# Neighbourhood attention in an encoder trunk: two key blocks laid over each other in PSUM, put apart again by GpSimd, and two PSUM pools in the other order

## The chip, the cores and the metric

The kernel runs on one core of a Trainium2 chip. The engines that matter are TensorE (PE in the profile, its weight loads PEld), VectorE (DVE), ScalarE (ACT), GpSimd (POOL) and SyncE (SP, which here issues most DMAs). The metric is the device time of one execution in microseconds (us); lower is better.

## The reference, cut to what matters

The trunk has two layers over 1024 tokens of width 1024, in float32. Layer 0 uses mixer A, layer 1 mixer B. The change touches mixer A: attention of 16 heads of 64 on a grid of 16 rows by 64 columns, in which each query sees a window of 8 rows and 16 columns of keys, clamped at the edges.

```python
def mixer_a(h, w_in, rpb, w_out):
    proj = h @ w_in
    q, k, v, gate = jnp.split(proj, 4, axis=-1)
    ...
    def row_block(args):                       # one grid row of queries
        kg = jnp.take(k, flat, axis=2)...      # the window's 8 x 16 keys
        sc = jnp.einsum('bhqd,bhqnd->bhqn', qb, kg) * scale
        sc = sc + bias                         # learned, by row and column offset
        pr = jax.nn.softmax(sc, axis=-1)
        return jnp.einsum('bhqn,bhqnd->bhqd', pr, vg)
    ...
    return (o * jax.nn.silu(gate)) @ w_out

for i in range(2):
    x = x + (mixer_a if i == 0 else mixer_b)(rms_norm(x, g[i]), ...)
    x = x + sigmoid(rms_norm(x, pg[i]) @ w_gate[i]) * (p[i] @ w_proj[i])
```

## The kernel before

**Stages.** The program runs mixer A (with the first layer's norm and projections), then `dense_phase(0)` (output projection, per-layer embedding gate), mixer B, and `dense_phase(1)`. Each stage opens its own PSUM pools; as pools are closed and opened, the banks of the eight pass from one stage to the next, and the first tile in a bank waits for the last reader of the tile that was there.

**Tiles of mixer A.** A token tile holds 128 tokens: all 16 grid rows of 8 neighbouring columns. So tile j's queries need keys of tiles j-1, j and j+1 alone. Every value is split into a high and a low part (fp32r), so a product is three matmuls, or two where the parts are stacked in the 128 rows of the array.

**One step** is one head h and one query tile j; there are 16 x 8 = 128 steps, and in 96 of them (j = 1 to 6) there are three key tiles. For a step the kernel issues:
- `f_S`: two matmuls of 384 columns give the scores in PSUM; one DVE operation (L741) adds the table `TB[h]` (bias and mask, negated) to them, writes `sp` to SBUF and keeps the smallest value;
- `f_E`: ACT takes the exponential of `sp` (L750) with the row's sum;
- `f_T`: PE transposes `sp` in blocks of 128 (L758, three of them, two at the edges), ACT copies the result from PSUM to `PTh` (L761) and DVE writes the rest to `PTl` (L762);
- `f_AV`: for key tile kb, PE multiplies the transposed weights of up to three query tiles with `V`.

**Order of the work.** In step n the list `att` takes `f_T(n)`, `f_E(n+1)`, `f_S(n+2)` and `f_AV(n-2)`, in that order. `mix` spreads between them the dense matmuls of the next head's query and key projection (`qk_items`) and of the gate. In heads 3, 7 and 11 the projection of V for the next four heads rides along with `f_AV`. After the last step two `f_AV` remain.

**Work held back.** `post.add(k, f)` holds a piece of work back by k ticks of the walk through the list, `later.add` by steps. The query and key projection of a head's half leaves PSUM by ACT into `th`; then at the ticks `QD = (2, 5, 8)` the functions `one`, `two` and `three` of `qk_evac` make `QS`, `KA` and `KB`: ACT copies (L685, L686), DVE subtractions (L689, L690) and two DVE copies from partitions 64 to 127 to partitions 0 to 63 (L691 for `KA`, L694 for `KB`).

**The end of a head** (`head_end`): when a half of a head's output is complete, ACT and DVE take it to `Y`, the row sums' reciprocals go through DRAM and come back by DMA as `rb`, and after the odd head of a pair `fin` multiplies on GpSimd `Y` by the gate (L563) and by `rb` (L564); then `split` writes high and low parts (ACT L560, DVE L561).

**GpSimd in mixer A** has the table of the next head (L716, five operations a head, at j = 1), the two multiplications of `fin`, and DMA issues of the weight sums (L632, `jobs`, at most one a step). Its queue runs in order: an operation that waits holds back all that follow.

**The dense phase's pools.** `ps_t` (transposes, 4 banks) is opened before `ps_d` (products, 4 banks), so `ps_t` has banks 0 to 3 and `ps_d` banks 4 to 7. Mixer A has its `d` in banks 0 and 1, `s` in 2 and 3, `t` in 4 and 5, `o` in 6 and 7. Mixer B has `d` in bank 0, `s` in 1 to 4, `t` in 5 and 6, `o` in 7.

Of the kernel before, what the change touches and what calls it, by code (L numbers as in the profile page):

```python
# [44 lines left out]
QD = (2, 5, 8)  # L45
# [42 lines left out]
def lay_out(inp):  # L88
# [47 lines left out]
    mask = np.where(ok, 0.0, BIG).astype(np.float32)  # L136

# [8 lines left out]
    def swap(v):  # L146
# [6 lines left out]
        "mask": mask, "rope": np.stack([cosT, sinT], axis=1),  # L153
# [5 lines left out]
def trunk(ctx, tc, x, wts, rpb, gains, hgains, mask, rope, gain0, out):  # L159
# [482 lines left out]
    def mixer_a():  # L642
        jobs = weight_sums()
        with ExitStack() as es:
# [6 lines left out]
            MK = one.tile([128, 5, 128], F32, name="MK")  # L651

# [19 lines left out]
            def qk_evac(h, hf):  # L672
                def evac(ps):
                    if hf == 0:
                        QS[h] = qkp.tile([128, 1024], F32R, name="QS")
                        KA[h] = qkp.tile([128, 1024], F32R, name="KA")
                        KB[h] = qkp.tile([128, 1024], F32R, name="KB")
                    s = slice(hf * 512, (hf + 1) * 512)
                    lo, hi = slice(0, 64), slice(64, 128)
                    qs, ka, kb = QS[h], KA[h], KB[h]  # L680
                    raw = sb.tile([128, 512], F32, name="th", bufs=2)
                    act.activation(raw, ps, AF.Copy)

                    def one():
                        act.activation(qs[lo, s], raw[lo], AF.Copy, scale=-0.125)  # L685
                        act.activation(ka[hi, s], raw[hi], AF.Copy)  # L686

                    def two():
                        dve.scalar_tensor_tensor(qs[hi, s], raw[lo], -0.125, qs[lo, s], op0=ALU.mult, op1=ALU.subtract)  # L689
                        dve.tensor_tensor(kb[hi, s], raw[hi], ka[hi, s], ALU.subtract)  # L690
                        dve.tensor_copy(ka[lo, s], ka[hi, s])  # L691

                    def three():
                        dve.tensor_copy(kb[lo, s], kb[hi, s])  # L694
                    for i, f in enumerate((one, two, three)):
                        if h == 0:
                            f()
                        else:
                            post.add(QD[i], f)
                return evac  # L700
# [19 lines left out]

            def near(j):
                return max(j - 1, 0), min(j + 1, NT - 1)

            def f_S(h, j):
                k0, k1 = near(j)
                n = (k1 - k0 + 1) * 128
# [3 lines left out]
                mm(ps[:, :n], qt, KA[h][:, ks], True, False)  # L730
                mm(ps[:, :n], qt, KB[h][:, ks], False, True)
# [14 lines left out]
            def f_E(h, j):  # L746
                k0, k1 = near(j)
                n = (k1 - k0 + 1) * 128
                sp, mn = SP[h, j]
                act.activation(sp[:, :n], sp[:, :n], AF.Exp, bias=mn, scale=-1.0, accum_out=RS[h][:, j:j + 1])  # L750

            def f_T(h, j):
                k0, k1 = near(j)
                m = k1 - k0 + 1
                sp, _ = SP.pop((h, j))
                ps = psT.tile([128, 4, 128], F32, name="t")
                for i in range(m):
                    pe.transpose(ps[:, i], sp[:, i * 128:(i + 1) * 128], ident)  # L758
                f0 = k0 * 3 + (j - k0 + 1)
                sl = slice(f0, f0 + 2 * m - 1, 2)  # L760
                act.activation(PTh[:, sl], ps[:, :m], AF.Copy)  # L761
                dve.tensor_tensor(PTl[:, sl], ps[:, :m], PTh[:, sl], ALU.subtract)  # L762
# [127 lines left out]
            sync.dma_start(MK, mask)  # L890
            for c in range(8):
                sync.dma_start(U[:, c], rpb[:, :, 7 - c:31 - c])
# [28 lines left out]
            PTh = ptp.tile([128, NT * 3, 128], F32R, name="PTh")  # L921
            PTl = ptp.tile([128, NT * 3, 128], F32R, name="PTl")
# [10 lines left out]
            f_E(0, 0)  # L933
            f_S(0, 1)
# [9 lines left out]
            for h in range(NH):  # L944
                att = []
                for j in range(NT):
                    n = h * NT + j
                    def head(h=h, j=j):
                        later.tick()
                        if j == 1 and h + 1 < NH:  # L950
                            table(h + 1)
                        if h >= 1 and j != 1 and jobs:
# [9 lines left out]
                    if n >= 2:  # L962
                        att += av_and_v(*steps[n - 2])
# [5 lines left out]
                if h == NH - 1:  # L969
                    att += [(lambda: f_AV(NH - 1, NT - 2), CA[4]), (lambda: f_AV(NH - 1, NT - 1), CA[4])]  # L970
# [517 lines left out]
    def dense_phase(l):  # L1488
        with ExitStack() as es:
            one = es.enter_context(tc.tile_pool(name="done", bufs=1))  # L1490
            ps_t = es.enter_context(tc.tile_pool(name="dpt", bufs=4, space=PSUM))
            ps_d = es.enter_context(tc.tile_pool(name="dps", bufs=4, space=PSUM))
# [250 lines left out]
NAMES = ["x", "wts", "rpb", "gains", "hgains", "mask", "rope", "gain0"]  # L1743
# [15 lines left out]
```

## Time and profile before

| | |
|---|---|
| median of 3 runs (lowest to highest) | 1531.45 us (1528.62 to 1531.79) |
| the profiled execution's own time, its span | 1530.75 us, 1528.9 us |
| granted TensorE clock, mean over the span | 0.998 |
| busy, share of the span: PE, PEld | 98%, 86% |
| DVE, ACT, POOL | 72%, 59%, 20% |
| mixer A's steps | about 60 to 530 us |
| `dense_phase(0)` | about 530 to 710 us |
| mixer B | about 710 to 1340 us |
| `dense_phase(1)` | about 1340 us to the end |

A group's row gives line, engine, operation, output and inputs by name, shape and count, then the busy time in us and the mean of one in ns, then the idle time before them and what ended it. In a timeline row stand the start in us, the duration in us, and in brackets the idle time before it and its releaser. Matmuls are pipelined: the duration of one runs from its start to the modelled end of its results, so two neighbours overlap, and what one costs on PE is the distance from its start to the next one's.

### The profile page before, as it was taken

What the parts mean: (1) busy time and instruction counts of PE and PEld (TensorE: products, weight loads), DVE (VectorE), ACT (ScalarE), POOL (GpSimd) and SP (SyncE); (2) the same over time, 40 slices, a digit from 0 to 9 for tenths busy, and PEclk for the clock granted to TensorE, in tenths of its full rate; (3) what the DMA queues carried; (4) which work ended last, traced back from release to release, by engine and by line L of the source; (5) the groups of instructions that cost most, each with busy time, mean ns of one, the idle gap of its engine ahead of it and who ended that gap; (6) DMA issues with size and microseconds to landing.
All of it is one profiled execution on the core that took longest, in us unless ns stands there. A gap on an engine that the chain in (4) does not pass through costs nothing.

```text
span 1528.9 us, 24361 instructions
## 1 busy us (share of the span) xinstructions
PE 1499.4 (98%) x8976; PEld 1314.0 (86%) x8976; DVE 1102.1 (72%) x2091; ACT 899.4 (59%) x1801; POOL 304.4 (20%) x413
## 2 busy tenths in 40 slices
PE   8999999999999999999999999999999999999997
PEld 8888988988988888888988889989899888878786
DVE  7566576477477599767887786777877877789856
ACT  6565465466366635433467676676767777745432
POOL 1222232142112000010222132453141300000022
PEclk9999999999999999999999999999999999999999
DMA  8325355272122962262210111111101122763123
GB/s 256 119 95 140 83 142 162 63 165 85 36 87 66 334 247 97 90 201 79 77 49 21 32 39 50 46 32 43 58 27 47 37 77 70 234 225 115 67 88 134
DMA packets 91096, 157.22 MB, mean 103 GB/s; under 512 B 18144, under 2 KB 54112, under 8 KB 90464
## 3 DMA queue, kind: packets, MB, share of 16 engines
q1 hardware_dynamic: 85824, 139.66, 27.9%
q0 software_dynamic: 2560, 8.39, 3.2%
q10 hardware_dynamic: 2592, 7.61, 1.4%
q8 instruction: 71, 1.16, 0.3%
q14 instruction: 49, 0.40, 0.1%
HBM read 125.10 MB, written 50.83 MB: 115 GB/s over the span
## 4 chain that ended last, share of the span: by engine, by line
PE 80%; DVE 11%; ACT 5%; issue 2%; DMA 1%; SPq 0%; ACTq 0%; DVEq 0%
PE d L317 50%; PE o L317 10%; PE s L317 8%; PE t L1214 6%; PE t L758 3%; DVE PTl L1217 2%; PE t L317 1%; PE t L467 1%; DVE mn L1198 1%; DVE xn L1541 1%; ACT PTh L1216 1%; ACT P L1204 1%; ACT wh L226 1%; DVE X L1437 1%; DVE HTl L1383 1%
## 5 line engine op out<-in xcount | busy, mean ns | idle before, releaser
L317 PE MATMUL d<-wh,HTh 128*128 128x256 f32 (+1 forms) x1032 | 343.3, 335 | 6.0 <-DVE HTl L469 2.3
L317 PE MATMUL d<-wh,HTl 128*128 128x256 f32 (+1 forms) x1032 | 338.3, 330 | 0.3 <-DVE HTl L469 0.3
L317 PE MATMUL d<-wl,HTh 128*128 128x256 f32 (+1 forms) x1032 | 337.0, 328 | 0.0
L1217 DVE TENSOR_TENSOR PTl<-t,PTh 128x512 fp32r<-128x512 f32 x256 | 164.4, 683 | 111.4 <-ACT PTh L1216 111.1
L317 PEld LDWEIGHTS d<-wh,HTh 128*128 128x128 f32 x1032 | 195.1, 190 | 25.8 <-DVE HTl L469 2.5
L317 PEld LDWEIGHTS d<-wl,HTh 128*128 128x128 f32 x1032 | 194.9, 190 | 19.0
L317 PEld LDWEIGHTS d<-wh,HTl 128*128 128x128 f32 x1032 | 195.1, 190 | 18.7 <-DVE HTl L469 0.5
L317 PE MATMUL d<-HTh,wh 128*128 128x512 f32 x504 | 206.0, 409 | 0.0
L317 PE MATMUL d<-HTh,wl 128*128 128x512 f32 x504 | 198.3, 394 | 0.0
L317 PE MATMUL d<-HTl,wh 128*128 128x512 f32 x504 | 197.6, 392 | 0.0
L1204 ACT ACTIVATE P<-s,mn 128x1024 f32<-128x1024 f32 x128 | 142.8, 1116 | 67.5 <-DVE mn L1198 66.7
L1216 ACT ACTIVATE PTh<-t 128x512 fp32r<-128x512 f32 x256 | 139.7, 593 | 45.1 <-PE t L1214 44.6
L1198 DVE TENSOR_REDUCE mn<-s 128x1 f32<-128x1024 f32 x128 | 154.7, 1209 | 12.3 <-PE s L317 12.3
L1214 PE MATMUL t<-ident,P 128*128 128x128 f32 x1024 | 137.2, 275 | 4.8 <-DVE PTl L1217 1.7
L317 PE MATMUL s<-KA,QS 128*128 128x512 f32 (+2 forms) x384 | 133.7, 402 | 0.0
L1214 PEld LDWEIGHTS t<-ident,P 128*128 128x128 f32 x1024 | 114.7, 140 | 20.1 <-DVE PTl L1217 12.6
L231 DVE TENSOR_TENSOR wl<-wstage,wh 128x1024 fp32r<-128x1024 f32 x78 | 101.7, 1308 | 34.7 <-ACT wh L226 34.2
L317 PE MATMUL s<-KB,QS 128*128 128x512 f32 (+2 forms) x384 | 121.8, 371 | 0.0
L317 PE MATMUL o<-PTh,V 128*128 128x256 f32 (+2 forms) x672 | 118.9, 288 | 1.2 <-DVE Y L483 0.9
L317 PE MATMUL o<-PTl,V 128*128 128x256 f32 (+2 forms) x672 | 119.1, 288 | 0.1
L762 DVE TENSOR_TENSOR PTl<-t,PTh 128x384 fp32r<-128x384 f32 (+1 forms) x128 | 66.6, 520 | 71.3 <-ACT PTh L761 70.1
L317 PEld LDWEIGHTS d<-HTh,wl 128*128 128x128 f32 x504 | 94.7, 188 | 21.6
(237 smaller groups left out, 2700.9 us busy)
## 6 DMA issues: line engine op xcount, KB each, us to landing
wstage<-in_wts SPq DMA_DIRECT2D x88, 512.0 KB
pp<-ppD SPq DMA_DIRECT2D x32, 256.0 KB
X<-in_x SPq DMA_DIRECT2D x15, 512.0 KB
rb<-rD SPq DMA_DIRECT2D x56, 128.0 KB
ppD<-th SPq DMA_DIRECT2D x20, 256.0 KB
tD0t<-in_wts SPq DMA_DIRECT2D x16, 256.0 KB
tD1t<-in_wts SPq DMA_DIRECT2D x16, 256.0 KB
xD<-X SPq DMA_DIRECT2D x8, 512.0 KB
```

Of the source, the lines that this page charges most:

```text
L226: act.activation(hi, s, AF.Copy)
L231: eng.tensor_tensor(lo[:, c:c + n], s[:, c:c + n], hi[:, c:c + n], ALU.subtract)
L317: pe.matmul(ps, a, b, start=first, stop=last, skip_group_check=True)
L467: pe.transpose(ps[:, k], xn[:, (4 * c + k) * 128:(4 * c + k + 1) * 128], ident)
L758: pe.transpose(ps[:, i], sp[:, i * 128:(i + 1) * 128], ident)
L762: dve.tensor_tensor(PTl[:, sl], ps[:, :m], PTh[:, sl], ALU.subtract)
L1198: dve.tensor_reduce(mn, ps, axis=AX.X, op=ALU.min)
L1204: act.activation(p, ps, AF.Exp, bias=mn, scale=-1.0, accum_out=RS[h, hf][:, t:t + 1])
L1214: pe.transpose(ps[:, i], p[:, k * 128:(k + 1) * 128], ident)
L1216: act.activation(PTh[:, ks, c], ps, AF.Copy)
L1217: dve.tensor_tensor(PTl[:, ks, c], ps, PTh[:, ks, c], ALU.subtract)
L1383: dve.tensor_tensor(al(t + m, c), src[m], ah(t + m, c), ALU.subtract)
```

## The change

**Overlay.** A key in tile j-1 (left) counts for a query only if its column within the tile is greater than the query's, a key in tile j+1 (right) only if it is smaller. For one pair of column numbers at most one of the two counts. The change uses this: after the scores' matmuls (still 384 columns) a new DVE operation copies the right block over the left one in PSUM, where a predicate (`SIDE[:, 2]`) says so (L747). The table of a head is joined in the same way, once a head (`join`, L726). The bias, the exponential, the transposes, `PTh` and `PTl` then handle 256 columns instead of 384 in the 96 inner steps; `sp` is 256 wide.

**Apart.** The transposed overlay lands in a staging slot of `PTh` and `PTl` (slots 24 and 25, by turns). Two GpSimd operations a step (L776, one for `PTh`, one for `PTl`) multiply it by two masks of ones and zeros into the two slots of the left and the right key tile. That is 192 operations more.

**AV later.** `f_AV` and the projection of V that rides with it run for step n-3 instead of n-2, and three `f_AV` remain after the last step. All that follows the end of a head comes one step later too.

**Query and key.** `QD` has five ticks instead of three. The two DVE copies across partitions (L691, L694 before) become ACT copies (L697), each at a tick of its own.

**Pools.** `ps_d` is opened before `ps_t`, so `ps_d` has banks 0 to 3 and `ps_t` banks 4 to 7.

The predicate tile `SIDE` (128 x 384) comes in by one more DMA at the start. Lines after the first hunk move down, by 1 to 20.

```diff
-QD = (2, 5, 8)
+QD = (2, 4, 6, 7, 9)
...
+    sides = np.stack([c[:, None] >= c[None, :], c[:, None] < c[None, :], c[:, None] > c[None, :]], axis=1).astype(np.float32)
...
+            SIDE = one.tile([128, 3, 128], F32, name="SIDE")
...
-                    def two():
+                    def low_q():
                         dve.scalar_tensor_tensor(qs[hi, s], raw[lo], -0.125, qs[lo, s], op0=ALU.mult, op1=ALU.subtract)
+
+                    def low_k():
                         dve.tensor_tensor(kb[hi, s], raw[hi], ka[hi, s], ALU.subtract)
-                        dve.tensor_copy(ka[lo, s], ka[hi, s])
-
-                    def three():
-                        dve.tensor_copy(kb[lo, s], kb[hi, s])
+
+                    def across(k):
+                        act.activation(k[lo, s], k[hi, s], AF.Copy)
+                    parts = (one, low_q, lambda: across(ka), low_k, lambda: across(kb))
...
+            def join(h):
+                dve.copy_predicated(TB[h][:, 1], SIDE[:, 2].bitcast(mybir.dt.int32), TB[h][:, 3])
...
-                    tb = TB[h][:, 1:4]
-                sp = sb.tile([128, 384], F32, name="sp", bufs=3)
+                    tb = TB[h][:, 1:3]
+                    dve.copy_predicated(ps[:, 0:128], SIDE[:, 2].bitcast(mybir.dt.int32), ps[:, 256:384])
+                sp = sb.tile([128, 256], F32, name="sp", bufs=3)
...
-                for i in range(m):
-                    pe.transpose(ps[:, i], sp[:, i * 128:(i + 1) * 128], ident)
-                f0 = k0 * 3 + (j - k0 + 1)
-                sl = slice(f0, f0 + 2 * m - 1, 2)
-                act.activation(PTh[:, sl], ps[:, :m], AF.Copy)
-                dve.tensor_tensor(PTl[:, sl], ps[:, :m], PTh[:, sl], ALU.subtract)
+                inner = 0 < j < NT - 1
+                for i in range(2):
+                    c = 1 - i if inner else i
+                    pe.transpose(ps[:, i], sp[:, c * 128:(c + 1) * 128], ident)
+                k0 = near(j)[0]
+                f0 = 3 * j + 1 if inner else k0 * 3 + (j - k0 + 1)
+                f1 = 3 * NT + j % 2 if inner else f0 + 2
+                sl = slice(f0, f1 + 1, f1 - f0)
+                act.activation(PTh[:, sl], ps[:, :2], AF.Copy)
+                dve.tensor_tensor(PTl[:, sl], ps[:, :2], PTh[:, sl], ALU.subtract)
+                if inner:
+                    def apart():
+                        for pt in (PTh, PTl):
+                            pool.tensor_tensor(pt[:, 3 * j - 1:3 * j + 4:4], pt[:, f1:f1 + 1].to_broadcast([128, 2, 128]), SIDE[:, :2],
+                                               ALU.mult)
+                    apart()
...
+            join(0)
...
+                        if j == 5 and h + 1 < NH:
+                            join(h + 1)
...
-                    if n >= 2:
-                        att += av_and_v(*steps[n - 2])
+                    if n >= 3:
+                        att += av_and_v(*steps[n - 3])
...
-                    att += [(lambda: f_AV(NH - 1, NT - 2), CA[4]), (lambda: f_AV(NH - 1, NT - 1), CA[4])]
+                    att += [(lambda k=k: f_AV(NH - 1, k), CA[4]) for k in range(NT - 3, NT)]
...
-            ps_t = es.enter_context(tc.tile_pool(name="dpt", bufs=4, space=PSUM))
             ps_d = es.enter_context(tc.tile_pool(name="dps", bufs=4, space=PSUM))
+            ps_t = es.enter_context(tc.tile_pool(name="dpt", bufs=4, space=PSUM))
```

How this moves instructions shows on two engines. The first is ScalarE in head 6, from the exponential of tile 4 on (`sp` is the exponential, `PTh` the copy of the transposed weights, `rb<-Y` the high part that `split` writes after `fin`, `wh` the high part of a weight, `QS`, `KA`, `KB` the next head's query and keys). Before:

```order
L750 ACTIVATE sp,rs<-sp,mn 128x384
L560 ACTIVATE rb<-Y 128x512
L761 ACTIVATE PTh<-t 128x3x128
L750 ACTIVATE sp,rs<-sp,mn 128x384
L682 ACTIVATE th<-d 128x512
L226 ACTIVATE wh_2727<-wstage 128x1024
L685 ACTIVATE QS<-th 64x512
L686 ACTIVATE KA<-th 64x512
L761 ACTIVATE PTh<-t 128x3x128
L750 ACTIVATE sp,rs<-sp,mn 128x384
```

And of the change, at the same place:

```order
L758 ACTIVATE sp,rs<-sp,mn 128x256
L697 ACTIVATE KB<-KB 64x512
L771 ACTIVATE PTh<-t 128x2x128
L758 ACTIVATE sp,rs<-sp,mn 128x256
L684 ACTIVATE th<-d 128x512
L227 ACTIVATE wh_2812<-wstage 128x1024
L561 ACTIVATE rb<-Y 128x512
L687 ACTIVATE QS<-th 64x512
L688 ACTIVATE KA<-th 64x512
L771 ACTIVATE PTh<-t 128x2x128
L758 ACTIVATE sp,rs<-sp,mn 128x256
```

The high part `rb<-Y` has moved from ahead of one exponential to the group of `wh`, `QS` and `KA` ahead of a later one, and a copy across partitions (`KB<-KB`) stands where it was.

The second is GpSimd in head 8, from the table of head 9 on (`tb`), with the two multiplications of `fin` (`Y`) and the DMA issues of the weight sums (`tD1t`). Before:

```order
L716 TENSOR_TENSOR tb<-MK,u 128x128 x5
L563 TENSOR_TENSOR Y<-Y,G 128x512
L564 TENSOR_TENSOR Y<-Y,rb 128x512
L632 DMA tD1t_84<-in_wts 64x1024 x2
L632 DMA tD1t_86<-in_wts 64x1024
L563 TENSOR_TENSOR Y<-Y,G 128x512
L564 TENSOR_TENSOR Y<-Y,rb 128x512
```

And of the change:

```order
L720 TENSOR_TENSOR tb<-MK,u 128x128 x5
L776 TENSOR_TENSOR PTh<-PTh,SIDE 128x2x128
L776 TENSOR_TENSOR PTl<-PTl,SIDE 128x2x128
L633 DMA tD1t_84<-in_wts 64x1024
L776 TENSOR_TENSOR PTh<-PTh,SIDE 128x2x128
L776 TENSOR_TENSOR PTl<-PTl,SIDE 128x2x128
L564 TENSOR_TENSOR Y<-Y,G 128x512
L565 TENSOR_TENSOR Y<-Y,rb 128x512
L633 DMA tD1t_84<-in_wts 64x1024
L776 TENSOR_TENSOR PTh<-PTh,SIDE 128x2x128
L776 TENSOR_TENSOR PTl<-PTl,SIDE 128x2x128
L633 DMA tD1t_86<-in_wts 64x1024
```

The new pairs stand between the table, the DMA issues and the multiplications of `fin`; the multiplication by `rb`, which waits for a DMA, now has pairs behind it that PE's `f_AV` waits for.

More of the change, by code (lines that the diff above doesn't have):

```diff
@@ L698, in evac @@
                         else:
-                            post.add(QD[i], f)
+                            post.add(at, f)
                 return evac
@@ L746, in f_E @@
             def f_E(h, j):
[L747 to L748 removed]
+                n = 256
                 sp, mn = SP[h, j]
@@ L920, in mixer_a @@
             ptp = es.enter_context(tc.tile_pool(name="ptp", bufs=1))
-            PTh = ptp.tile([128, NT * 3, 128], F32R, name="PTh")
-            PTl = ptp.tile([128, NT * 3, 128], F32R, name="PTl")
+            PTh = ptp.tile([128, NT * 3 + 2, 128], F32R, name="PTh")
+            PTl = ptp.tile([128, NT * 3 + 2, 128], F32R, name="PTl")
             for d in qk_items(0):
```

20 lines of the change are left out of this document (10 added, 10 removed).

## The prediction, made before the change was run

> **What bounds the kernel now.** I read the busy time by stretch first. A row is the stretch, its length, and per engine the busy us with the number of instructions, then the granted clock, the DMA share and GB/s.
>
> ```profile
> 60.00:530.00 470.00, 468.44 (x2686) 409.19 (x2685) 299.49 (x665) 276.60 (x618) 106.10 (x130) 1.00 0.41 119
> 530.00:560.00 30.00, 28.54 (x127) 23.62 (x127) 28.23 (x41) 13.99 (x21) 0.00 (x0) 1.00 0.75 286
> 700.00:800.00 100.00, 95.33 (x689) 88.24 (x688) 78.89 (x208) 51.53 (x115) 19.23 (x32) 1.00 0.19 62
> ```
>
> In mixer A's steps (60 to 530 us) PE has work for 468.4 of 470 us at full clock, VectorE for 299 (64%), ScalarE for 277 (59%), GpSimd for 106 (23%). The chain of waits in 40 to 560 us says the same:
>
> ```profile
> by line: PE d L317 70.8%; PE o L317 8.2%; PE s L317 7.5%; PE t L758 7.4%; PE t L317 2.1%; ACT wh L226 1.3%; ACT sp L750 0.6%; ACT PTh L761 0.4%; ACT th L682 0.3%; issue 0.3%; ACT V L668 0.2%; PE t L502 0.2%; DVE QS L689 0.1%; DVE KB L690 0.
> ```
>
> PE's own issue sets the time here; the transposes L758 are 7.4% of the chain and other engines only show as splinters. So an instruction taken from PE is worth what it costs there, and work added elsewhere is free as long as PE does not wait for it.
>
> **What a transpose costs on PE.** A group's duration overlaps its successor; the distance of starts counts. Four rows of head 6 and 7, transposes and the scores' matmul behind them, with a fifth for the length of a head:
>
> ```profile
> 227.66 0.38 PE L758 MATMUL t<-ident,sp 128*128 128x128 f32 x2
> 252.17 0.38 PE L758 MATMUL t<-ident,sp 128*128 128x128 f32 x2
> 252.31 0.42 PE L317 MATMUL s<-KA,QS 128*128 128x384 f32 x1
> 258.18 0.49 PE L758 MATMUL t<-ident,sp 128*128 128x128 f32 x3
> 258.43 0.42 PE L317 MATMUL s<-KA,QS 128*128 128x384 f32 x1
> ```
>
> Two transposes hold PE for 252.31 - 252.17 = 0.14 us, three for 258.43 - 258.18 = 0.25 us. One costs 0.11 us, not the 0.275 us of the group's mean. Head 6 runs from 227.66 to 252.17, 24.5 us for 8 steps, 3.06 us each. The change drops one transpose in 96 steps: **96 x 0.11 = 10.6 us less on PE**. The scores' matmuls stay 384 wide, `f_AV` keeps its columns; nothing else on PE changes. That is the first term.
>
> **VectorE and ScalarE, by form.** The columns are line, operation, shapes and count, then busy us and mean ns of one.
>
> ```profile
> L758 PE MATMUL t<-ident,sp 128*128 128x128 f32 x352 | 60.2, 275 | 1.4 <-ACT sp L750 1.0
> L750 ACT ACTIVATE sp<-sp,mn 128x384 f32<-128x384 f32 x96 | 58.9, 613 | 8.2 <-DVE mn L741 7.5
> L762 DVE TENSOR_TENSOR PTl<-t,PTh 128x384 fp32r<-128x384 f32 x96 | 53.4, 556 | 62.5 <-ACT PTh L761 61.7
> L741 DVE CUSTOM_DVE_ANT_0 sp<-s,tb 128x384 f32<-128x384 f32 x96 | 52.5, 547 | 10.9 <-PE s L317 10.6
> L761 ACT ACTIVATE PTh<-t 128x384 fp32r<-128x384 f32 x96 | 47.1, 490 | 55.8 <-PE t L758 54.9 <-issue 0.3
> L686 ACT ACTIVATE KA<-th 64x512 fp32r<-64x512 f32 x32 | 20.1, 629 | 0.6
> L750 ACT ACTIVATE sp<-sp,mn 128x256 f32<-128x256 f32 x32 | 16.2, 506 | 9.1 <-DVE mn L741 9.1
> L694 DVE CAST KB<-KB 64x512 fp32r<-64x512 f32 x32 | 15.9, 498 | 0.9
> L691 DVE CAST KA<-KA 64x512 fp32r<-64x512 f32 x32 | 15.1, 471 | 1.0
> L741 DVE CUSTOM_DVE_ANT_1 sp<-s,tb 128x256 f32<-128x256 f32 x32 | 13.4, 419 | 0.8 <-PE s L317 0.3
> L762 DVE TENSOR_TENSOR PTl<-t,PTh 128x256 fp32r<-128x256 f32 x32 | 13.2, 412 | 8.8 <-ACT PTh L761 8.4
> L761 ACT ACTIVATE PTh<-t 128x256 fp32r<-128x256 f32 x32 | 12.2, 381 | 8.5 <-PE t L758 8.2
> L509 DVE RECIPROCAL r<-rs 128x4 f32<-128x4 f32 x64 | 10.9, 170 | 0.0
> ```
>
> VectorE saves in a step 547 - 419 = 128 ns (L741) and 556 - 412 = 144 ns (L762), and pays the copy by predicate of 128 columns in PSUM, which has no row. It takes at least what the smallest operation takes (170 ns, L509) and at most what the 384-wide L741 takes (547 ns). L741 costs 128 ns for 128 columns, so at 128 columns it would be 419 - 128 = 291 ns; I take 0.29 us. A step then changes by 0.29 - 0.27 = +0.02 us, 96 x 0.02 = 2 us (at 0.17: -10, at 0.55: +26). The 64 copies across partitions leave VectorE, 32 x 0.471 + 32 x 0.498 = 31 us, and 16 `join` add 16 x 0.29 = 5 us. VectorE ends at 299 + 2 - 31 + 5 = 275 us (299 at the upper bound), under PE's 458: zero on the path. The copy stands between the scores and L741, but the exponential of those scores is a whole step (3 us) further on, more than the 0.55 us of the upper bound; without that cover each of the 96 steps would pay up to 0.55 us.
>
> ScalarE saves 613 - 506 = 107 and 490 - 381 = 109 ns in each of 96 steps, 20.7 us, and takes over 64 copies at some 0.63 us (L686, same shape), 40 us: 277 + 20 = 297 of 460 us. On average that hides too. But the order in its queue matters, and one place has no cover. ScalarE from step (6,4) to (6,6), and the transposes' weight load behind it:
>
> ```profile
> 237.77 0.62 ACT L560 ACTIVATE rb<-Y 128x512 fp32r<-128x512 f32 x1
> 242.52 1.05 ACT L226 ACTIVATE wh<-wstage 128x1024 fp32r<-128x1024 f32 x1
> 245.26 0.62 ACT L750 ACTIVATE sp<-sp,mn 128x384 f32<-128x384 f32 x1
> 245.79 0.18 ACT L750 ACTIVATION_READ_ACCUMULATOR sp<-sp,mn 128x1 f32 x1
> 246.02 0.31 PEld L758 LDWEIGHTS t<-ident,sp 128*128 128x128 f32 x3 [0.31 <-ACT sp L750]
> ```
>
> After `wh`, `QS`, `KA` and `PTh` the exponential ends at 245.97 and its transposes begin at 246.02: no slack. `fin` comes later in the change, and its `rb<-Y` (0.62 us), which stood in a loose place (237.77), now stands right in this row of work. The stretch gets 0.62 - 0.11 - 0.11 = +0.40 us, and PE arrives 0.11 us sooner. With 0.05 us of slack PE waits 0.40 + 0.11 - 0.05 = 0.46 us, in the seven heads that carry it (2, 4, ... 14): **+3.2 us**. Lower bound 0 (the tick falls elsewhere), upper bound 7 x 0.62 = 4.3.
>
> **GpSimd.** The 192 multiplications write 128 x 256 from two SBUF inputs. Nearest rows, and one wait:
>
> ```profile
> L716 POOL TENSOR_TENSOR tb<-MK,u 128x128 f32<-128x128 f32 x80 | 48.7, 748 | 181.9 <-DVE mn L741 168.8 <-DMA u<-U 13.2
> L563 POOL TENSOR_TENSOR Y<-Y,G 128x512 f32<-128x512 f32 x28 | 40.8, 1458 | 128.1 <-DVE Y L483 128.1
> L564 POOL TENSOR_TENSOR Y<-Y,rb 128x512 f32<-128x512 f32 x28 | 36.2, 1294 | 145.3 <-DMA rb<-rD 144.9
> L1066 POOL TENSOR_TENSOR qt<-qt,ss 128x256 f32<-128x256 f32 x32 | 20.2, 660 | 33.8 <-DVE ss L336 28.2 <-DVE r L509 5.4
> 197.82 1.29 POOL L564 TENSOR_TENSOR Y<-Y,rb 128x512 f32<-128x512 f32 x1 [10.78 <-DMA rb<-rD]
> ```
>
> Lower bound 0.66 us (L1066), upper 1.46 us (L563, twice the size); I take 0.8, near the row of equal size. A head then needs 12 x 0.8 = 9.6 us, the table 5 x 0.75 = 3.7, in even heads `fin` 2 x (1.46 + 1.29) = 5.5: 18.8 of 24 us. It keeps up. The danger is order: L564 waits for the DMA of `rb` (up to 10.8 us, 144.9 in all), which cost nothing while only DMA issues stood behind it. Now the pair of the next tile stands there, and `f_AV` needs that pair two steps (6.1 us) after its transposes; with `rb` one step later than now, 6.1 - 3.1 = 3 us remain for L564 and the pair, 1.29 + 1.6 = 2.9. About even: I take **+1.0 us** in sum, bounds 0 and 7 x 1.3 = 9.1 (the second `fin` of each even head late by a whole L564). That `f_AV` comes one step later is what makes this room; it costs PE nothing, since the same matmuls run in the gaps of the same dense work.
>
> **The pools.** The first product of mixer B:
>
> ```profile
> 708.40 0.60 ACT L1598 ACTIVATE th<-d 128x512 f32<-128x512 f32 x1 [2.10 <-PE d L317]
> 710.37 0.69 DVE L469 TENSOR_TENSOR HTl<-t,HTh 128x512 fp32r<-128x512 f32 x1
> 711.11 0.39 PE L317 MATMUL d<-wh,HTh 128*128 128x256 f32 x1 [2.31 <-DVE HTl L469]
> ```
>
> Mixer B's `d` takes bank 0. It was a `t` bank of the dense phase, so the matmul waits until VectorE has read the last transposes (710.37 + 0.69 = 711.06). In the change bank 0 was a `d` bank, whose last reader is the L1598 that ends at 709.00; the matmul can start at about 709.1: **-2.0 us** (bounds -2.3 and 0, if a chain further on eats it). At the entry to `dense_phase(0)` it is alike:
>
> ```profile
> 530.14 0.60 ACT L606 ACTIVATE G<-d 128x512 f32<-128x512 f32 x1 [1.27 <-PE d L317]
> 530.72 0.69 DVE L536 TENSOR_TENSOR Y<-Y,t 128x512 f32<-128x512 f32 x1
> 531.51 0.47 PE L317 MATMUL d<-wh,HTh 128*128 128x512 f32 x1 [1.46 <-ACT G L606]
> ```
>
> The bank was mixer A's `t`, read last by L536 (to 531.41). Now it is mixer A's `d`, read last by L606 (to 530.74): start at about 530.85, **-0.7 us**. The second half's VectorE chain there comes later than now in a stretch where VectorE is full (28.2 of 30 us), so 0 is the other bound, and a loss of 1.5 us (the length of today's gap) is possible.
>
> **Sum.** -10.6 + 3.2 + 1.0 - 2.0 - 0.7 = -9.1 us on the profiled execution's 1530.75: 1521.7. That execution lies 0.7 us under the median of the runs shown; against the median it is 1522.3, and I say **1522**.
>
> **Rivals.** *GpSimd is too slow and PE waits for it* (slower). At the upper bound, 1.46 us, an even head needs 17.5 + 3.7 + 5.5 = 26.7 us against a head of 24.5 - 0.65 = 23.85 us. Heads 2, 6, 10 and 14, which have no V projection to stretch them, lose 2.9 us each, 11.4; with the late second `fin` (+2) the sum is -9.1 + 13.4 = +4.3, **1535**. It decides from (23.85 - 9.2) / 12 = 1.22 us an operation. For it: L563 takes 1.46; against: it has twice the elements, and L1066 has 0.66.
>
> *ScalarE's copies eat the gain* (no change). The two copies across a head's `KB` wait for VectorE's L690 and stand ahead of an exponential. If both meet a place as tight as the one above, in 15 heads, each costs 0.63 - 0.22 - 0.05 = 0.36 us, 30 x 0.36 = 10.8 in place of 3.2: -1.5, **1530**. For it: VectorE's producer can be late:
>
> ```profile
> 236.24 1.29 POOL L563 TENSOR_TENSOR Y<-Y,G 128x512 f32<-128x512 f32 x1 [1.59 <-DVE Y L483]
> 236.91 1.16 DVE L689 SCALAR_TENSOR_TENSOR QS<-th,QS 64x512 fp32r<-64x512 f32 x1
> ```
>
> L689, with two inputs in SBUF, ends at 238.07, soon after the GpSimd operation it started under (237.53). With 192 more of them such meetings multiply. The Trainium skill, "SBUF — State Buffer", section "Who interferes with whom", has it as a rule: a VectorE instruction with two SBUF inputs and a GpSimd instruction that reads SBUF exclude each other for the whole instruction, by order of issue. By that rule, which these two rows agree with, every L690 could be a GpSimd operation late, and this rival would gain. Against it: the copies have ticks of their own, most exponentials stand loose, and 297 of 460 us is not much. That the dropped transposes were hidden anyway would also end near 1530; the distances of 0.14 and 0.25 us speak against it.
>
> *Nothing collides* (a larger gain): `rb<-Y` meets a loose place and GpSimd is always in time: -10.6 - 2.0 - 0.7 = -13.3, **1518**.
>
> **Chances.** Forecast 0.50 (own range 1518 to 1527); GpSimd late 0.20; eaten 0.16; nothing collides 0.14. A measurement of this kernel can tell about 0.2%, 3.1 us, from no change. Faster: 0.50 + 0.14 + 0.03 of the eaten case = 0.67; same 0.13; slower 0.20. The range 1516 to 1537 holds all four times, with room for the copy's unknown price; some 2 in 10 lie outside.
>
> **What would show it.** Right: L758's successor has 256 transposes, PE's busy time in the steps falls by about 10 us, and the stretch 60 to 530 us shrinks by 6 to 7. In even heads ScalarE's `rb<-Y` stands ahead of a short PE idle at the transposes. The pair on GpSimd takes 0.7 to 0.9 us each, and PE's waits that name GpSimd sum to about 1 us. The 2.3 us ahead of mixer B's first product fall under 0.5. Wrong: GpSimd's operations at 1.2 us or more, PE's `o` matmuls waiting for them in every even head, VectorE's copy above 0.55 us, or transposes that wait for the exponential in most steps.

## The result, and the profile after

| | before | changed |
|---|---|---|
| median of 22 runs each | 1530.91 us | 1532.88 us |
| ratio, 95% interval | | 1.0017 (1.001 to 1.0024) |
| profiled execution, its span | 1530.75, 1528.9 us | 1534.67, 1532.9 us |

The change did not make the kernel faster; by the ratio it made it slower by about 2.6 us (by the medians 2.0), a little under what the prediction had called measurable in one comparison, but clear of noise with so many runs. The forecast was 1522 us. One of the changed kernel's 22 runs took 2977.56 us, at a granted clock of 1.00; the ratio leaves it out, and no trace shows its cause.

The busy time by stretch, in the same three stretches as before:

```profile
60.00:530.00 470.00, 457.72 (x2567) 395.21 (x2566) 281.12 (x708) 293.08 (x674) 250.00 (x322) 1.00 0.42 116
530.00:560.00 30.00, 29.10 (x131) 23.33 (x130) 25.03 (x37) 11.62 (x19) 0.00 (x0) 1.00 0.83 313
700.00:800.00 100.00, 97.52 (x694) 89.93 (x692) 79.31 (x215) 51.38 (x118) 19.35 (x32) 1.00 0.23 77
```

The stretch from 60 to 530 us has a fixed length, so the fall of PE's busy time in it, from 468.4 to 457.7 us, is its idle time seen from the other side: 12.3 us now, 1.6 before. It does not show the 10.6 us of the first term; what a dropped transpose is worth as work shows in run 7. The steps themselves, by the timeline from the first transposes to the last, take 466.2 us (61.02 to 527.20) instead of 461.9 (61.64 to 523.55). Where PE stands idle is in the groups by line, first of the changed kernel and in the last row of the kernel before. The columns are line, engine, operation, output and inputs, shapes and count, then busy us and mean ns, then the idle time before them and what ended it:

```profile
L776 POOL TENSOR_TENSOR PTl<-PTl,SIDE 128x256 fp32r<-128x256 f32 x96 | 80.8, 842 | 5.7 <-DVE PTl L772 5.7
L776 POOL TENSOR_TENSOR PTh<-PTh,SIDE 128x256 fp32r<-128x256 f32 x96 | 76.3, 795 | 211.0 <-ACT PTh L771 210.8
L758 ACT ACTIVATE sp<-sp,mn 128x256 f32<-128x256 f32 x128 | 65.0, 508 | 10.8 <-DVE mn L750 9.4
L766 PE MATMUL t<-ident,sp 128*128 128x128 f32 x256 | 50.4, 278 | 11.7 <-ACT sp L758 11.7
L520 ACT ACTIVATE Y<-o 64x512 f32<-64x512 f32 x64 | 37.9, 594 | 15.3 <-DMA yD0l<-Y 10.1 <-PE o L318 2.0 <-PE s L318 1.5
L747 DVE COPY_PREDICATED s<-SIDE,s 128x128 f32<-128x128 int32 x96 | 27.7, 288 | 24.1 <-PE s L318 23.6
L726 DVE COPY_PREDICATED tb<-SIDE,tb 128x128 f32<-128x128 int32 x16 | 11.0, 685 | 0.1
L519 ACT ACTIVATE Y<-o 64x512 f32<-64x512 f32 x64 | 38.0, 594 | 24.4 <-PE o L317 19.4 <-issue 4.2
```

PE's wait ahead of the transposes was 1.4 us in the kernel before; it is 11.7 us now, all of it for ScalarE's exponential. What was saved came back as 10.3 us of waiting at the very operation that had been thinned out. (By the distance of starts each of these waits costs PE about 0.17 us more than its row says, 0.57 for 0.40 us in head 2, which is part of why the steps even got longer.) `Y<-o`, ScalarE's copy of a finished half of a head's output, waits 10.1 us for a DMA (the store of `Y`); before no such wait was in its row. GpSimd's pair costs 0.80 and 0.84 us and no PE row names it; the copy by predicate costs 0.288 us. So these additions were priced well; what hurt was elsewhere.

Four timeline rows of head 5 show how the DMA reaches PE (the last column is the idle time before and its releaser):

```profile
204.47 0.59 ACT L520 ACTIVATE Y<-o 64x512 f32<-64x512 f32 x1 [3.60 <-DMA yD0l<-Y]
205.09 0.38 ACT L771 ACTIVATE PTh<-t 128x256 fp32r<-128x256 f32 x1
205.37 0.50 ACT L758 ACTIVATE sp<-sp,mn 128x256 f32<-128x256 f32 x1
206.01 0.44 PE L766 MATMUL t<-ident,sp 128*128 128x128 f32 x2 [1.92 <-ACT sp L758]
```

`Y` has two buffers. The new half may not be written before the half of two earlier has gone to DRAM. ScalarE stands 3.60 us at that copy, and the exponential is behind it in ScalarE's queue; PE comes to the transposes of that exponential and waits 1.92 us. The same happens in heads 7 and 9: 2.62 and 3.62 us at the copy, 0.97 and 1.95 us on PE. Together PE loses 4.8 us so.

At mixer B's entry and at the dense phase's the pools did what was forecast:

```profile
534.32 0.60 ACT L607 ACTIVATE G<-d 128x512 f32<-128x512 f32 x1 [1.92 <-PE d L318]
534.97 0.50 PE L318 MATMUL d<-wh,HTh 128*128 128x512 f32 x1 [0.30 <-ACT G L607]
714.17 0.60 ACT L1618 ACTIVATE th<-d 128x512 f32<-128x512 f32 x1 [2.11 <-PE d L318]
714.82 0.39 PE L318 MATMUL d<-wh,HTh 128*128 128x256 f32 x1 [0.25 <-ACT th L1618]
```

The wait of 2.31 us at mixer B fell to 0.25, that of 1.46 us at the dense phase to 0.30.

### The profile page after: what moved, and what is told of

The parts are those of the page before. It is cut to its first block, busy times and chain, and to the rows that moved or that the text cites. A ratio compares the mean times of both kernels' runs of the same rounds, so it can differ in the third digit from the quotient of the medians.

```text
span 1532.9 us, 24679 instructions
## 1 busy us (share of the span) xinstructions
PE 1492.9 (97%) x8880; PEld 1301.9 (85%) x8880; DVE 1084.6 (71%) x2139; ACT 920.3 (60%) x1865; POOL 448.0 (29%) x605
## 4 chain that ended last, share of the span: by engine, by line
PE 38%; DVE 9%; ACT 4%; issue 2%; ACTq 0%; DVEq 0%
PE d L318 18%; PE o L318 7%; PE s L318 6%; PE t L1234 6%; DVE PTl L1237 1%; DVE mn L1218 1%; ACT PTh L1236 1%; ACT P L1224 1%; PE t L318 1%; DVE xn L1561 1%; PE t L1188 0%; DVE X L1457 0%; DVE QS L1198 0%; DVE wl L232 0%; ACT wh L227 0%
## 5 line engine op out<-in xcount | busy, mean ns | idle before, releaser
L776 POOL TENSOR_TENSOR PTh<-PTh,SIDE 128x256 fp32r<-128x256 f32 x96 | 76.3, 795 | 211.0 <-ACT PTh L771 210.8
L232 DVE TENSOR_TENSOR wl<-wstage,wh 128x1024 fp32r<-128x1024 f32 x78 | 98.1, 1259 | 32.2 <-ACT wh L227 32.0
```

What stands on the lines that cost most here:

```text
L232: eng.tensor_tensor(lo[:, c:c + n], s[:, c:c + n], hi[:, c:c + n], ALU.subtract)
L776: pool.tensor_tensor(pt[:, 3 * j - 1:3 * j + 4:4], pt[:, f1:f1 + 1].to_broadcast([128, 2, 128]), SIDE[:, :2], ALU.mult)
```

## The experiments

Each run has its own runs of the kernel before on the same chip; its ratio is to those. "Lag" below is the step by which `f_AV` runs behind the transposes.

**1. A third buffer for Y.**

```diff
-            Y = sb.tile([128, 512], F32, name="Y", bufs=2)
+            Y = sb.tile([128, 512], F32, name="Y", bufs=3)
```

> The changed kernel with a third buffer for Y, so that ScalarE's copy of o into Y no longer waits for the store of the Y of two halves earlier. Theory (that wait is where about half of the gain went): the three long waits of PE behind it at the second steps of heads 5, 7 and 9 (2.1, 1.1 and 2.1 us) go, and the time falls 5.3 us below the changed kernel's, to 1527 to 1528, ratio to before 0.997 to 0.999. Rival (PE only waits for something else instead): within 1 us of the changed kernel, ratio 1.001 to 1.002.

Measured: 1527.91 us, ratio 0.9982 (0.9973 to 0.9991), 5 us under the changed kernel. In its timeline head 5 reads so:

```profile
200.45 0.60 ACT L520 ACTIVATE Y<-o 64x512 f32<-64x512 f32 x1
201.83 0.50 ACT L758 ACTIVATE sp<-sp,mn 128x256 f32<-128x256 f32 x1
203.46 0.38 PE L766 MATMUL t<-ident,sp 128*128 128x128 f32 x2
```

The copy has no wait, the exponential ends 1 us ahead of its transposes and PE has none. Over all heads PE's wait at the transposes falls from 11.7 to 7.0 us:

```profile
L766 PE MATMUL t<-ident,sp 128*128 128x128 f32 x256 | 50.3, 278 | 7.0 <-ACT sp L758 6.9
```

The theory held: this wait alone took about half of the 9.1 us that were forecast, and without it the change is faster than the kernel before.

**2. The pools, taken back from the change and put alone into the kernel before.** The edit is the order of two lines:

```diff
-            ps_d = es.enter_context(tc.tile_pool(name="dps", bufs=4, space=PSUM))
             ps_t = es.enter_context(tc.tile_pool(name="dpt", bufs=4, space=PSUM))
+            ps_d = es.enter_context(tc.tile_pool(name="dps", bufs=4, space=PSUM))
```

> The changed kernel with the dense phase's pools in the order of before. By the prediction (2.0 us at mixer B's first product, 0.7 us at the dense phase's start) the time rises by 2.7 us, ratio 1.003 to 1.004. Theory after seeing the trace (2.1 us won at mixer B, 2.1 us lost within the first dense phase, 1.2 us lost at the start of the second): 0 to 1.5 us faster than the changed kernel, ratio 1.000 to 1.002. The 2.3 us wait ahead of mixer B's first product must come back in either case.

> The kernel before with only the dense phase's pools in the new order. By the prediction -2.7 us, ratio 0.998. Theory (given back in the dense phases): -0.5 to +1 us, ratio 0.9997 to 1.0007; the waits that are new in the first dense phase (0.6 to 0.7 us at X and xn) and at the start of the second (0.9 us) must show here if they come from the pools.

Measured: the changed kernel with the old order takes 1538.91 us, ratio 1.0058 (1.0045 to 1.0071); the kernel before with the new order 1527.77 us, ratio 0.9982 (0.9973 to 0.9991). The prediction's 2.7 us is right for the kernel before, and the theory formed after seeing the trace, that the dense phases give it back, fell in both runs: with the pools alone the waits at X and xn in the first dense phase do not show, only that of 0.7 us at the start of the second. The wait of 2.3 us ahead of mixer B's first product came back with the old order. In the changed kernel the order is worth 0.0041 of the time, some 6 us. Its old order shows why, at the start of the dense phase:

```profile
537.36 0.69 DVE L537 TENSOR_TENSOR Y<-Y,t 128x512 f32<-128x512 f32 x1
538.15 0.76 PE L318 MATMUL d<-wh,HTh 128*128 128x512 f32 x1 [3.90 <-issue]
```

and right behind it, by the busy time of a stretch (the third number from the end is the granted clock):

```profile
538.00:540.00 2.00, 1.85 (x5) 1.49 (x6) 1.30 (x4) 1.91 (x3) 0.00 (x0) 0.50 0.00 1
```

The profile names no releaser for this wait (`issue`); that it is L537 is read from the time, since the matmul starts 0.10 us after L537's end, as it did in the kernel before. With the later `f_AV` VectorE finishes the last head later, so the matmul waits 3.90 us instead of 1.46, and the granted clock after that wait is 0.50 for two microseconds. The new order takes PE out of that chain.

**3. The late `f_AV` alone, in the kernel before.**

```diff
-                    if n >= 2:
-                        att += av_and_v(*steps[n - 2])
+                    if n >= 3:
+                        att += av_and_v(*steps[n - 3])
...
-                    att += [(lambda: f_AV(NH - 1, NT - 2), CA[4]), (lambda: f_AV(NH - 1, NT - 1), CA[4])]
+                    att += [(lambda k=k: f_AV(NH - 1, k), CA[4]) for k in range(NT - 3, NT)]
```

> The kernel before with only f_AV and the V projection one step later. The prediction priced this at nothing: within 1 us. Theory (a head's end comes a step later but its split moves by two, so the copy into Y meets the store): waits of Y<-o for the store in heads 4, 6 and 8 of 2 us or more and a time 3 to 5 us longer, ratio 1.002 to 1.003.

Measured: 1548.48 us, ratio 1.011 (1.0093 to 1.0127): 17 us slower, more than three times what even the theory expected. Two of its groups by line:

```profile
L758 PE MATMUL t<-ident,sp 128*128 128x128 f32 x352 | 60.9, 277 | 8.9 <-ACT sp L750 8.7
L519 ACT ACTIVATE Y<-o 64x512 f32<-64x512 f32 x64 | 37.9, 594 | 7.3 <-DMA yD0l<-Y 3.0 <-PE o L317 2.5 <-issue 0.3
```

and two timeline rows of its last head:

```profile
522.29 0.60 ACT L606 ACTIVATE tb<-d 128x512 f32<-128x512 f32 x1 [4.04 <-DMA ppD<-tb]
522.93 0.59 PE L317 MATMUL d<-wh,KA 128*128 128x512 f32 x1 [2.11 <-ACT tb L606]
```

The wait at the transposes grows from 1.4 to 8.9 us. By the timeline only 0.9 us of it stand behind the store of `Y`: the copy into `Y` waits 1.79 us in head 3 and 1.19 us in head 7, not 2 us or more in heads 4, 6 and 8 as the theory had it. At the seventh steps of heads 2, 4, 6, 8, 10 and 12, where `rb<-Y` has moved to, stand 2.9 us; at the sixth steps of heads 4, 8 and 12, where the exponential waits 1.69 us for VectorE's minimum, 2.7 us; in the first head 2.3 us. In the last head ScalarE waits 4.04 us for a buffer that is being stored and PE 2.11 us with it. The first product of the dense phase waits 3.90 us (at 547.05), here too instead of 1.46. And the granted clock falls behind three of PE's waits, of 2.11, 3.90 and 2.30 us:

```profile
523.00:527.00 4.00, 4.00 (x12) 3.19 (x13) 1.62 (x4) 3.10 (x7) 0.00 (x0) 0.57 0.93 268
548.00:552.00 4.00, 4.00 (x14) 3.21 (x13) 3.97 (x6) 1.37 (x3) 0.00 (x0) 0.69 0.22 50
```

The third fall is at 728 to 732 us, to 0.57. By the clock in stretches of 2 us the three cost about 1.7 us each, 5 us in all (an estimate). So 7.5 us at the transposes, 2.1 in the last head, 2.4 at the dense phase and 5 by the clock are some 17 of the 18.4 us by which the spans of the two profiled executions differ. This is the part of the change that costs, and the store is the least of it here.

**4. The split three ticks earlier.** `YS = (11, 11)` becomes `YS = (8, 11)`, so that `rb<-Y` stands right behind an exponential; `Y` keeps two buffers.

> The changed kernel with fin's split (rb<-Y on ScalarE) three ticks earlier, behind an exponential instead of among wh, QS and KA; Y keeps two buffers. Theory: the waits of about 0.55 us at the seventh steps of the even heads (six, 3.2 us) go, and since the store of Y leaves over 2 us sooner most of the 5.3 us behind Y<-o go too: 6 to 8.5 us under the changed kernel, ratio to before 0.9965 to 0.998. Rival (both waits only move on to the next ScalarE operation): 0 to 2 us, ratio 1.0005 to 1.002.

Measured: 1527.86 us, ratio 0.9979 (0.997 to 0.9987), 5 to 6 us under the changed kernel, at the small end of the theory's band. Its rows:

```profile
L766 PE MATMUL t<-ident,sp 128*128 128x128 f32 x256 | 50.2, 278 | 6.4 <-ACT sp L758 6.1
L520 ACT ACTIVATE Y<-o 64x512 f32<-64x512 f32 x64 | 37.9, 594 | 4.5 <-PE o L318 2.0 <-DMA yD0l<-Y 0.9
```

`Y<-o` waits for the store 0.9 us instead of 10.1. It is the same wait as in run 1, reached from its other end. The store that head 5 waits for is issued no sooner, at 198.68 us instead of 198.43, but it stands elsewhere in SyncE's order: in the changed kernel the load of a weight (`wstage`, 512 KB) is issued 1.0 us ahead of it, here and in the kernel before 1.2 us behind it. The stores that heads 7 and 9 wait for change places with such a load in the same way. That the place ends the store sooner is read from these rows; no run tries it apart. The changed kernel has a wait of 0.34 to 0.40 us at the transposes of the seventh step in each of heads 2, 4, 6, 8, 10 and 12 (0.50 to 0.57 us by the distance of starts). In heads 2, 6 and 10 it fell to 0.12 us or less; in heads 4, 8 and 12 it stayed. So `rb<-Y` was the cause in half of them only.

**5. The copies across partitions back on VectorE** (with three `Y` buffers): the functions `two` and `three` and `QD = (2, 5, 8)` as before.

> The changed kernel with three Y buffers and the copies across partitions back on VectorE at the old three ticks. Theory (ScalarE's copies, each ahead of an exponential, make the waits of 0.65 and 0.46 us in steps 3 and 4 of heads 4, 8 and 12, 3.3 us in all): 2 to 4 us under the run with three Y buffers, ratio to before 0.9955 to 0.997. Rival (VectorE, 31 us fuller, is late with the scores): as with three Y buffers or slower, ratio 0.998 to 1.001, with VectorE's mn named at ScalarE's exponentials.

Measured: 1541.69 us, ratio 1.0074 (1.0062 to 1.0087), 14 us slower than run 1. The theory fell; the rival's direction held, by far more than it had said.

```profile
L757 ACT ACTIVATE sp<-sp,mn 128x256 f32<-128x256 f32 x128 | 64.9, 507 | 47.1 <-DVE mn L749 46.4
L765 PE MATMUL t<-ident,sp 128*128 128x128 f32 x256 | 50.9, 280 | 17.1 <-ACT sp L757 16.1
L693 DVE CAST KA<-KA 64x512 fp32r<-64x512 f32 x32 | 25.4, 793 | 0.8
L696 DVE CAST KB<-KB 64x512 fp32r<-64x512 f32 x32 | 18.2, 568 | 0.9
```

The exponentials wait 46.4 us for VectorE's minimum, against 9.4 in the changed kernel, and PE waits 17.1 us at the transposes, against 7.0 in run 1. And the copies themselves, 471 and 498 ns in the kernel before, take 793 and 568 ns once GpSimd works more than twice as much. The edit moves the copies and their ticks together; which of the two counts for how much is not shown.

**6. The same part alone in the kernel before.**

> The kernel before with only the query and key part of the change (five ticks, the two copies across partitions on ScalarE). Theory (the copies on VectorE cost only where the rest of the change makes VectorE's work come late; ScalarE's copies make the waits of steps 3 and 4 in heads 4, 8 and 12): 1 to 4 us slower than before, ratio 1.0005 to 1.003. Rival (the copies on VectorE hold back the scores in the kernel before too): 1 us or more faster, ratio under 0.9995.

Measured: 1533.55 us, ratio 1.0021 (1.0012 to 1.003), 3 us slower, as the theory said. So this part, copies and ticks together, costs 3 us by itself and is worth 14 us once the other parts are there.

**7. A third transpose put back**, its result unread (with three `Y` buffers):

```diff
+                if inner:
+                    pe.transpose(ps[:, 2], sp[:, 0:128], ident)
```

> The changed kernel with three Y buffers and a third transpose in each of the 96 inner steps, whose result nothing reads. By the prediction's first term it costs 96 x 0.11 = 10.6 us over the run with three Y buffers, ratio to before 1.004 to 1.006. Rival (part of the drop only lengthened PE's waits): 3 to 7 us, ratio 1.000 to 1.003.

Measured: 1535.62 us, ratio 1.0032 (1.002 to 1.0043), 7.7 us over run 1; between the full 10.6 and the rival's 3 to 7, and nearer to the latter, though the two intervals allow some 5 to 10 us. The new transposes and the old ones in its groups:

```profile
L766 PE MATMUL t<-ident,sp 128*128 128x128 f32 x256 | 50.0, 277 | 5.1 <-ACT sp L758 4.9
L768 PE MATMUL t<-ident,sp 128*128 128x128 f32 x96 | 26.1, 272 | 0.0
```

As work the first term is right: over the whole program PE's busy time is 1501.2 us, in run 1 1490.7, so the 96 transposes add 10.5 us. PE's wait at the old transposes is 5.1 us, in run 1 it is 7.0: some of the added work fell into time in which PE stood idle anyway. About three quarters of the first term are real time.

**8. `f_AV` back at lag 2 in the changed kernel** (with three `Y` buffers), so that it follows GpSimd's pair by one step only.

> The changed kernel with three Y buffers and f_AV (and the V projection) back at step n-2. Theory (GpSimd's pair for a tile ends some 3.2 us after its transposes, a step is 2.3 or 3.7 us, so f_AV waits for GpSimd in some of the steps by up to 1 us, but a head's end keeps its old place): between 5 us under and 5 us over the run with three Y buffers, with PE's o naming GpSimd. Rival of the prediction (the late f_AV is what makes the room): PE waits 1 us or more in most inner steps, 50 us or more, ratio above 1.03.

Measured: 1529.49 us, ratio 0.9992 (0.9983 to 1.0002), about 1.5 us over run 1, with intervals that overlap.

```profile
L318 PE MATMUL o<-PTh,V 128*128 128x256 f32 x576 | 91.8, 286 | 2.1 <-DVE Y L484 0.9 <-POOL PTh L776 0.9 <-ACT PTh L1236 0.2
L318 PE MATMUL o<-PTl,V 128*128 128x256 f32 x576 | 90.6, 284 | 2.9 <-POOL PTl L776 2.7
L318 PE MATMUL o<-PTl,V 128*128 128x384 f32 x64 | 22.1, 346 | 2.4 <-POOL PTl L776 2.4
L766 PE MATMUL t<-ident,sp 128*128 128x128 f32 x256 | 49.5, 275 | 2.3 <-ACT sp L758 2.2
```

PE now does wait for GpSimd (0.9 + 2.7 + 2.4 us here, two smaller groups of 1.7 us beside them, 7.7 us in all), and since the time hardly differs, some 6 us must be won back by the earlier end of a head. The last row shows 4.7 of them: PE's wait at the transposes is 2.3 us, in run 1 it is 7.0. The late `f_AV` is a fair trade for the overlay, no gift.

**9. The change without the overlay**: the kernel before with the late `f_AV`, the new query and key part and the new pools.

> The changed kernel without the overlay: three blocks are transposed, no copy by predicate, no multiplications on GpSimd; late f_AV, the new query and key part and the new pools stay, two Y buffers. Theory (the overlay is worth what the third transposes cost in the other run, 7 to 8 us, a little less for its own additions): 5 to 8 us slower than the changed kernel, ratio to before 1.005 to 1.007. Rival (the overlay's additions on VectorE and GpSimd pay back what the transposes save): within 2 us of the changed kernel, ratio 1.000 to 1.003.

Measured: 1542.03 us, ratio 1.0075 (1.0062 to 1.0087), 0.0058 or 9 us over the changed kernel. So the overlay by itself, with its additions on VectorE and GpSimd, is worth 9 us, a little above the theory's band, whose end lies within the interval; what surrounds it costs 11. Tried alone in the kernel before, the three surrounding parts came to 17, 3 and -3 us, 17 in all, so they do not simply add up.

**10. A mended version**: three `Y` buffers, `YS = (8, 11)`, lag 2 in head 15 alone, the new pool order in the first dense phase alone.

```diff
-                    if n >= 3:
+                    if n >= 3 and h < NH - 1:
                         att += av_and_v(*steps[n - 3])
+                    if h == NH - 1:
+                        for k in ((n - 3, n - 2) if j == 0 else (n - 2,)):
+                            att += av_and_v(*steps[k])
...
+            pools = {}
+            for name in ("dps", "dpt") if l == 0 else ("dpt", "dps"):
+                pools[name] = es.enter_context(tc.tile_pool(name=name, bufs=4, space=PSUM))
+            ps_d, ps_t = pools["dps"], pools["dpt"]
```

> The changed kernel with three Y buffers, the split three ticks earlier, f_AV back at step n-2 in head 15 alone, and the new pool order in the first dense phase alone. Theory: 5 us as with three Y buffers, 1.2 us for the split, 3.6 us at the end of mixer A and in the first dense phase, 0.9 us at the start of the second: 9 to 11 us under the changed kernel, 1521 to 1524, ratio to before 0.994 to 0.996. Rival (PE's waits move on): 1526 to 1528, ratio 0.997 to 0.998.

Measured: 1522.62 us, ratio 0.9951 (0.9937 to 0.9964), inside the theory's band. It beats both kernels. Its wait at the transposes is still 6.5 us:

```profile
L766 PE MATMUL t<-ident,sp 128*128 128x128 f32 x256 | 50.3, 278 | 6.5 <-ACT sp L758 6.2
```

**11. The late `f_AV` in the kernel before, mended in the same way** (three `Y` buffers, the earlier split, lag 2 in head 15; old pools, no overlay).

> The kernel before with late f_AV as in the run that took 18 us more, but with three Y buffers, the split three ticks earlier, and f_AV back at step n-2 in head 15. Old pools, old query and key part, no overlay. Theory (a late f_AV costs by what the end of a head meets: the store of Y, the split among ScalarE's weight work, and the last head's end ahead of the dense phase): most of the 18 us go, 1531 to 1536, ratio to before 1.000 to 1.004. Rival (the lateness itself costs, by PE's own order): 1540 or more, ratio above 1.006.

Measured: 1535.94 us, ratio 1.0031 (1.0019 to 1.0043). Of the 17 us 12 are gone and 5 stay, at the upper end of the theory's band. So most of the cost of lateness is in what a head's end meets, as the theory has it; the last head's share went by taking the lateness back there. The rest shows in the same row, 6.4 us of wait at the transposes against 1.4:

```profile
L758 PE MATMUL t<-ident,sp 128*128 128x128 f32 x352 | 60.5, 275 | 6.4 <-ACT sp L750 6.2
```

These waits are in the first head and in heads 4, 8 and 12, behind a V projection. In the latter the exponential of the sixth step waits 1.69 us for VectorE's minimum; why VectorE is late there, and what holds the first head up, was not tried apart.

## Why the prediction was wrong

**The step that failed** is the sentence on the late `f_AV`: "it costs PE nothing, since the same matmuls run in the gaps of the same dense work". PE's matmuls are indeed the same, but PE waits for what follows them. The end of a head hangs on the last `f_AV`: ScalarE's copy into `Y`, the row sums, `fin`, the split and the store. In the kernel before these stood where ScalarE's queue was loose and where the store had ended before `Y` was wanted again. The reading of the order rows did see that the split moves, and priced its 0.62 us; it did not ask what the split releases (the store), who waits for that (the `Y` buffer, two halves on), and what is queued behind the waiter (the exponential). Run 3 measures the step alone at 17 us. In the changed kernel PE's wait at the transposes, 11.7 us against 1.4 before, falls to 7.0 us with the third buffer (run 1) and from there to 2.3 us with `f_AV` back at lag 2 (run 8). So most of the 10.3 us that ate the gain hang on the late `f_AV`, about half of them by the store of `Y` (runs 1 and 4). For the other half the evidence is weaker, since in run 8 PE's new waits for GpSimd also leave ScalarE more time. A run with lag 2 and two buffers was not made. Nor did the prediction count with the clock, which costs about 5 of run 3's 17 us.

**By its other steps:**

- *96 x 0.11 = 10.6 us less on PE.* Right as work (10.5 us of busy time in run 7). As time 7.7 us by the same run: PE had idle time by then.
- *The split among `wh`, `QS` and `KA`, +3.2 us.* The waits came in six of the seven heads at 0.50 to 0.57 us by the distance of starts, 3.2 us in all. That this is the sum as forecast is in part luck, since there were six waits of 0.5 us and not seven of 0.46. And run 4 took the split away from there and three of them stayed, so the mechanism was half of it, and the larger cost of the same move, the store, was not in the sum.
- *GpSimd, 0.8 us an operation, +1.0 us.* The operation was right (0.80 and 0.84). No PE row names GpSimd in the changed kernel, so 0 instead of 1.0. Run 8 shows the reason given, that the late `f_AV` makes the room: without it those waits are there.
- *The copy by predicate, 0.29 us.* Measured 0.288 in PSUM. `join`, put at the same price, took 0.685, with both blocks in SBUF: 11 us on VectorE instead of 5.
- *The copies across partitions, zero on the path.* Wrong both ways: with their ticks 3 us of cost when moved alone (run 6), 14 us of worth inside the change (run 5). The average load of VectorE (275 of 458 us by the estimate) said nothing on it; the minimum that the exponential waits for is late by what stands in the queue at that moment.
- *The pools, -2.7 us.* Right in the kernel before, in both places (0.3 and 0.7 us of wait remain); the 0.7 us that it costs at the start of the second dense phase were not in the sum. In the changed kernel worth 6 us, since they also take PE out of a chain that the late `f_AV` had lengthened.

**The rivals.** None of the three was it. "ScalarE's copies eat the gain" gave nearly the right time, 1530 for 1533, and the right place, transposes that wait for the exponential. Its reason was wrong in the main: ScalarE's copies of `KB` do wait for VectorE's L694, 19.1 us in 18 places, but run 5 shows that with the copies back on VectorE the transposes wait longer. GpSimd's operations kept well under the 1.22 us from which the slower rival was to decide.

## What to carry to other kernels

A step that is moved takes with it everything that hangs on its completion: follow that chain to its last DMA, see what is issued ahead of that DMA, ask which buffer the DMA frees, who asks for that buffer next, and what is queued behind the one who asks. When work is removed from the engine that bounds a kernel, slack that was just enough before becomes a wait; look at the few places in which the bounding engine starts right behind its last input, and at averages of the others last. Parts of a change are not worth the same alone and together (the query and key part: -3 and +14 us, the pools: 2.7 and 6 us), so undo one part of the whole as well as doing one part alone.

## What the runs showed of the hardware that was not expected

The clock fell after short waits of PE. In the changed kernel PE waited 1.95 us up to 329.79 us, and then:

```profile
331.00:335.00 4.00, 4.00 (x13) 3.45 (x12) 1.03 (x4) 0.60 (x2) 1.93 (x3) 0.57 0.79 154
```

PE was busy throughout, with 13 matmuls where 21 to 23 are usual in 4 us, at a granted clock of 0.57. After the like wait of 1.92 us at 206.01 us the clock stayed at 1.00, so such a wait brings it at times only; by the distance of the matmuls' starts the cost was about 1.4 us (an estimate), in this one execution. Run 3 has three such falls, behind waits of 2.11, 3.90 and 2.30 us, and its four runs have a mean clock of 0.993 to 0.995 where the kernel before has 0.995 to 0.999. In the kernel before the wait of 2.31 us at 711.11 us brought none.

VectorE's single-input copies from SBUF to SBUF lengthened with GpSimd's load, for `KA` from 471 to 793 ns (run 5). By the timelines a copy that no GpSimd operation overlaps takes 0.42 us, in the kernel before and in run 5 alike. In run 5, 19 of the 32 copies of `KA` are overlapped by one and take 1.05 us in the mean, up to 1.42. The Trainium skill, "SBUF — State Buffer", section "Who interferes with whom", names `copy` and `cast` among the instructions that can take the port pair shared with GpSimd, when their operands allow it; these copies are `CAST` in the profile. These rows agree with it; the prediction had counted only the instructions with two inputs.
